# Reordering a top-256 search, three elementwise products and two loads in a two-layer trunk on Trainium2

## The chip, the cores and the metric

The kernel runs on one core of one Trainium2 chip. The metric is the device time of one execution in microseconds (us); lower is better. The number compared is the median of several executions.

## What is computed

The reference is a trunk of two layers over 1024 tokens of width 1024. Layer 0 projects its input into two groups of heads. Group A is RWKV-7 time mixing with eight heads of 64; group B is sparse attention with eight heads of 64, in which an indexer keeps for each query the 256 best keys. Layer 1 is gated linear attention. What the change touches is this part of layer 0, cut from the reference:

```python
kk = (k * kk_scale).reshape(Bn, T, H, Dh)
kk = kk / jnp.maximum(jnp.sqrt(jnp.sum(jnp.square(kk), -1, keepdims=True)), 1e-12)
k = k * (1.0 + (a - 1.0) * ka)
...
bonus = jnp.sum(r_h * k_h * rk, -1, keepdims=True) * v_h
...
score = jnp.where(adm[None], score, -jnp.inf)
vals, idx = lax.top_k(score, top_k)
```

The gates of both groups are SiLU of further columns of the same projection.

## The kernel before

**Projection.** Layer 0's input projection is computed 128 columns at a time: 21 column projections (`proj`, L527), each of 48 matmuls with 512 columns (three partial products L218 to L220 of split operands, two halves of the sequence) into one of two PSUM tiles called `dn`. A `dn` tile is drained by two instructions, one on ScalarE and one on VectorE: `shift_out` (L545 to L548) for r, k and v into one of three `sh` buffers, `gate` (L532 to L538) for a gate into the single `sg` buffer, which a DMA then stores to `d_gate`. TensorE can't start the projection after next before both drains are done. In the order of the program the last eight projections are v2, gate 4, gate 5, k3, v3, r3, gate 6 and gate 7; they are called the 14th to the 21st here. The digit of k3, v3 and r3 is the feature group j.

**Operands of the RWKV heads.** For each j from 0 to 3 and each half h of the sequence, `operands` (L606 to L634) makes the factors `ar` and `bk` of the chunked recurrence from r, k, the decays (L586 to L605) and the norms (`rn`, L570 to L584): L612, L615, L616, then kf (L619), k times kf (L620), L621, L622 and L623. `bk` is stored to `d_bk`, multiplied in place by PC (L628) and stored again to `d_bd`; r times k (L631, into a buffer called `kk`) feeds the `bonus` matmul (L637, one of 128x512 for each half), whose result VectorE takes up in L639. The table OG says for each kind of product up to which j it runs on GpSimd (POOL); on GpSimd a product runs in pieces of 128x256 by a helper whose line is L100.

**Search.** Beside the projections the threshold of the top 256 is searched for the score tiles 2 to 7 (128 queries each, 384 to 1024 keys). VectorE counts for tiles 3, 4 and 5 (`count_pass`, L738, 32 passes). ScalarE does tiles 2, 6 and 7 by sums of signs (`sign_pass`, L768 to L770): sixteen rounds on the upper 16 bits of the keys, a merge of both halves (nH, kd, L778 to L785), sixteen rounds on the rest. A round of one tile is a chain of three instructions. Then L794 to L801 turn the results into thresholds, for all of ScalarE's tiles at once, and the selection (L809 to L815) makes a mask from each tile in the order SELO.

**What sets the order.** A scheduler places the instructions of this part in each engine's queue; each engine then runs its queue strictly in that order. Behind the projection the second stage begins: the attention of tile i (`logits`: L915, L916 on TensorE, L917, L923 on VectorE, L925 on ScalarE; `weights`: L944) needs the queries `qT` of tile i, loaded by `load_q` (L899 to L902) into one of two buffers through SyncE's DMA queue (SP). Beside it run the recurrence's products (L1112 to L1116) on AT and BK, loaded through the same queue. Matmuls of this stage keep the order of the program.

Of the kernel before, what the change touches and what calls it, by code (L numbers as in the profile page):

```python
# [8 lines left out]
F32 = mybir.dt.float32  # L9
# [4 lines left out]
AF = mybir.ActivationFunctionType  # L14
ALU = mybir.AluOpType
# [6 lines left out]
P = 128  # L22
SEQ = 1024
# [36 lines left out]
PRE = ('', 'ab', 'cd!x', '0', '1lm', '', 'AB', 'CD!TX', '2', '3LM', '', '')  # L60
PO0 = 8
PINS = ()
SELO = (3, 4, 5, 2, 6, 7)
GNE = 'VVVV'
QSE = 'GG'
ATS = (2, 6, 7)
OG = (0, 0, 0, 0, 0, 0, 4, 4, 4, 0, 0)
ORD = (2, 3, 4, 9, 10, 5, 7, 11, 6, 8)
PG = [[], [0, 1], [], [], [2, 3], [4], [5], [6, 7], [], []]
RK1 = 0  # L70
# [11 lines left out]
def trunk(ctx: ExitStack, tc: tile.TileContext, x, positions, e_w_in, a_mu, a_w0, a_w2, a_a0, a_a2,  # L82
          a_kk_scale, a_ka, a_rk, a_gn_g, a_gn_b, b_kv_norm_g, b_wuk, b_wuv, e_w_out, o_w_in, c_g2,
          c_g_bias, c_norm_g, o_w_out, ln_g, ln_b, out, dbg=None, stop=None):
    nc = tc.nc
    V, A, G, PE = nc.vector, nc.scalar, nc.gpsimd, nc.tensor
    f32 = lambda ap: ap.bitcast(F32)
# [175 lines left out]
    d_q = dram.tile([NT, P, 8, P], F32, name="d_q")  # L263
# [79 lines left out]
    gt = gt_ctx.enter_context(tc.tile_pool(name="gt", bufs=1))  # L343
# [188 lines left out]
    def gate(z):  # L532
        g, j = divmod(z, 4)
        pt = proj((C_GB if g else C_GA) + j * P)
        o = gt.tile([P, SEQ], F32, name="sg")
        A.activation(o, pt, AF.Tanh, scale=0.5)
        V.scalar_tensor_tensor(o, o, 1.0, pt, op0=ALU.add, op1=ALU.mult)
        nc.sync.dma_start(d_gate[z], o)  # L538
# [22 lines left out]
    def st(name, w=SEQ, bufs=1, tag=None, pool=None):  # L561
        return (pool or t2).tile([P, w], F32, name=name, tag=tag or name, bufs=bufs)
# [149 lines left out]
    AT = ATS  # L712
# [4 lines left out]
    th = th_ctx.enter_context(tc.tile_pool(name="thr", bufs=1))  # L717
# [15 lines left out]
    def count_pass(b, last):  # L733


        for i in VT:
            z = col[i]
            V.tensor_scalar(junk[:, :P * (i + 1)], sc[:, rng(i)], Ff[:, z] if b < 31 else 0.0, None, op0=ALU.is_ge,  # L738
                            op1=ALU.add, accum_out=cnt[:, z])
        V.tensor_scalar(step, cnt, float(TOPK), float(1 << b) if b < 31 else -1.0, op0=ALU.is_lt, op1=ALU.mult)  # L740
        nxt = 1 << b >> 1
        if b == 31:
            V.tensor_scalar(F, step, nxt, None, op0=ALU.bitwise_xor)
        else:
            V.scalar_tensor_tensor(F, step, nxt, F, op0=ALU.bitwise_xor, op1=ALU.bitwise_xor)
# [14 lines left out]
    def half(i, z):  # L760
        return keys[i].bitcast(I16).rearrange("p (n z) -> p n z", z=2)[:, :, z]

    def sign_pass(b, data, c):


        for i in AT:
            zz = acol[i]
            A.activation(ajunk[:, :P * (i + 1)], data[i], AF.Sign, bias=c[:, zz], accum_out=cntA[:, zz])  # L768
            A.activation(sgA[:, zz], cntA[:, zz], AF.Sign, bias=odd[:, zz])
            A.activation(c[:, zz], sgA[:, zz], AF.Identity, scale=-0.5 * float(1 << b), bias=c[:, zz])  # L770
# [1 line left out]
    V.memset(Hc, 0.5)  # L772
    V.memset(Lc, 0.5)
    hi = {i: half(i, 1) for i in AT}
    for b in range(31, 15, -1):
        count_pass(b, False)
        sign_pass(b - 16, hi, Hc)
    V.tensor_scalar(nH, Hc, 131072.0, None, op0=ALU.mult)  # L778
    dist = {}
    for i in AT:  # L780
        n = P * (i + 1)
        d = th.tile([P, SEQ], F32, name="kd", tag="km", bufs=2)[:, :n]
        A.activation(d, hi[i], AF.Identity, scale=131072.0, bias=nH[:, acol[i]])
        dist[i] = keys[i].bitcast(F32)
        V.tensor_add(dist[i], d, half(i, 0))  # L785
    for b in range(15, -1, -1):
        count_pass(b, b == 0)
        sign_pass(b, dist, Lc)

    cand, nv = small("cand", NI), small("nv", NI)  # L790
    V.tensor_copy(cand[:, 0:ND], Ff)
# [107 lines left out]
    def load_q(i):  # L899
        if i < NT:  # L900
            QT_[i] = qp.tile([P, 8, P], F32R, name="qT", tag="qT", bufs=2)
            nc.sync.dma_start(f32(QT_[i]), d_q[i])  # L902

    def logits(i, h):

# [833 lines left out]
```

## Time and profile before

| what | value |
|---|---|
| median of 3 runs | 1267.45 us (1266.19 to 1272.92) |
| profiled execution | 1270.15 us, its span 1268.4 us |
| mean granted TensorE clock | 0.967 of full speed |
| TensorE busy | 1170.1 us, 92% of the span |
| VectorE, ScalarE, GpSimd busy | 60%, 50%, 34% of the span |

Times inside the profile are us from the start of the span. The span is 1.75 us shorter than the time of its own execution, and that execution was 2.7 us above the median. In the rows of the waits the last three numbers are the total wait, how often, and the longest.

### The profile page before, as it was taken

The numbers are of one execution on the slowest core, as the hardware profiler recorded it, in microseconds if no ns is written. First come the engines' busy times: TensorE is split into PE (matmuls) and PEld (weight loads), VectorE is DVE, ScalarE is ACT, GpSimd is POOL, SyncE is SP. The second block draws the span as 40 slices with busy tenths as digits, with TensorE's granted clock in tenths as the row PEclk, the third lists the DMA queues.
The fourth block names the chain that finished last, engine by engine and source line by source line (L and its number), as shares of the span: only waits on it lengthen the run. The fifth ranks groups of instructions, "written<-read, shape, count | busy, mean of one in ns | idle before, by whom it ended". The sixth has DMA issues, their size and how long they took to land.

```text
span 1268.4 us, 22109 instructions
## 1 busy us (share of the span) xinstructions
PE 1170.1 (92%) x8125; PEld 937.8 (74%) x8125; DVE 761.5 (60%) x1785; ACT 634.7 (50%) x1395; POOL 427.5 (34%) x741
## 2 busy tenths in 40 slices
PE   7998799989897968998988999999999999998997
PEld 6986587767675656777776777787788788886885
DVE  5245869989966666677776544882601034524666
ACT  5247859999882456666676421324811034413100
POOL 3233843536345333355454400513033130321000
PEclk9999899999998979999999999999999999998999
DMA  6102221535344475344454555852022020014221
GB/s 215 42 1 83 100 59 51 167 87 154 99 122 128 134 200 145 91 132 109 116 136 123 159 165 164 270 180 73 1 67 67 3 65 1 33 35 141 75 100 50
DMA packets 166096, 131.40 MB, mean 104 GB/s; under 512 B 61684, under 2 KB 139556, under 8 KB 165988
## 3 DMA queue, kind: packets, MB, share of 16 engines
q1 hardware_dynamic: 163152, 123.51, 33.4%
q10 hardware_dynamic: 2836, 6.49, 1.6%
q8 instruction: 64, 1.05, 0.4%
q14 instruction: 44, 0.36, 0.1%
HBM read 86.44 MB, written 42.99 MB: 102 GB/s over the span
## 4 chain that ended last, share of the span: by engine, by line
PE 61%; DVE 13%; ACT 10%; DMA 6%; issue 6%; POOL 4%; SPq 1%; DVEq 0%; ACTq 0%; POOLq 0%
PE op L858 7%; PE s L858 6%; PE dn L218 5%; PE dn L219 4%; PE dn L220 4%; DVE fe L738 3%; PE gt L242 2%; PE gt L240 2%; PE gt L241 2%; ACT fs L768 2%; PE s L944 2%; DMA wraw<-in_e_w_in_dram 2%; PE po L978 1%; PE tr L241 1%; PE tr L240 1%
## 5 line engine op out<-in xcount | busy, mean ns | idle before, releaser
L100 POOL TENSOR_TENSOR w<-qT,w 128x256 fp32r<-128x256 f32 x104 | 77.7, 782 | 210.1 <-ACT w L200 127.1
L218 PE MATMUL dn<-xh,chi 128*128 128x512 f32 x336 | 136.4, 406 | 8.7 <-DVE sh L547 7.3
L219 PE MATMUL dn<-xl,chi 128*128 128x512 f32 x336 | 133.9, 399 | 0.0
L220 PE MATMUL dn<-xh,clo 128*128 128x512 f32 x336 | 133.3, 397 | 0.0
L200 ACT CAST w<-qT 128x512 fp32r<-128x512 f32 x64 | 39.1, 622 | 106.1 <-PE dn L220 67.7
L218 PEld LDWEIGHTS dn<-xh,chi 128*128 128x128 f32 x336 | 64.2, 191 | 27.7 <-DVE sh L547 9.0
L738 DVE TENSOR_SCALAR_CACHE_REDUCE fe<-sc,F 128x512 bf16<-128x512 f32 (+2 forms) x93 | 81.6, 877 | 2.4
L219 PEld LDWEIGHTS dn<-xl,chi 128*128 128x128 f32 x336 | 64.2, 191 | 16.0 <-issue 3.1
L220 PEld LDWEIGHTS dn<-xh,clo 128*128 128x128 f32 x336 | 64.3, 191 | 14.1 <-issue 0.5
L100 POOL TENSOR_TENSOR clo<-craw,chi 128x256 fp32r<-128x256 f32 x84 | 73.2, 902 | 0.7
L858 PE MATMUL op<-w,yh 128*128 128x512 f32 x192 | 62.2, 411 | 1.4 <-ACT yh L1696 1.4
L925 ACT ACTIVATE w<-w,am 128x128 f32<-128x128 f32 (+7 forms) x64 | 49.6, 776 | 23.0 <-DVE am L923 22.8
L455 DVE SCALAR_TENSOR_TENSOR sc<-rl,wi_s,sc 128x384 f32<-128x384 f32 (+5 forms) x42 | 45.8, 1090 | 23.8 <-ACT rl L450 21.2
L944 PE MATMUL s<-ident,w 128*128 128x128 f32 x288 | 49.5, 298 | 9.2 <-ACT w L925 5.6
L100 POOL TENSOR_TENSOR vg<-vg,sg 128x256 f32<-128x256 f32 x32 | 23.7, 762 | 99.7 <-DVE vg L1661 53.6
L917 DVE CUSTOM_DVE_ANT_0 w<-s,bias_s 128x512 f32<-128x512 f32 (+1 forms) x80 | 45.3, 593 | 19.6 <-PE s L916 19.1
L228 POOL CAST chi<-craw 128x1024 fp32r<-128x1024 f32 x21 | 23.6, 1126 | 83.9 <-PE dn L219 54.6
L240 PE MATMUL gt<-w,hh 128*128 128x512 f32 x128 | 51.9, 406 | 0.0
L946 ACT COPY pT<-s 128x512 f32<-128x512 f32 x72 | 42.1, 586 | 18.7 <-PE s L944 17.6
L242 PE MATMUL gt<-w,hl 128*128 128x512 f32 x128 | 51.2, 400 | 0.0
L241 PE MATMUL gt<-w,hh 128*128 128x512 f32 x128 | 51.0, 399 | 0.0
L219 PE MATMUL dn<-hl,w 128*128 128x512 f32 x128 | 50.6, 395 | 0.0
(473 smaller groups left out, 3371.8 us busy)
## 6 DMA issues: line engine op xcount, KB each, us to landing
qT<-in_o_w_in_dram SPq DMA_DIRECT2D x48, 256.0 KB
craw<-in_e_w_in_dram SPq DMA_DIRECT2D x21, 512.0 KB
xt<-in_x_dram SPq DMA_DIRECT2D x8, 512.0 KB
d_q<-qiT SPq DMA_DIRECT2D x8, 512.0 KB
d_gate<-sg SPq DMA_DIRECT2D x8, 512.0 KB
d_ar<-ar SPq DMA_DIRECT2D x8, 512.0 KB
qT<-d_q SPq DMA_DIRECT2D x8, 512.0 KB
AT<-d_ar SPq DMA_DIRECT2D x32, 128.0 KB
```

What stands on the lines that cost most here:

```text
L100: return [f(out[:, a:min(n, a + w)], *(z[:, a:min(n, a + w)] for z in ins)) for a in range(0, n, w)]
L218: PE.matmul(pst, wh[:, cs], ah[:, k, sl], start=(k == 0), stop=False)
L219: PE.matmul(pst, wh[:, cs], al[:, k, sl], start=False, stop=False)
L220: PE.matmul(pst, wl[:, cs], ah[:, k, sl], start=False, stop=(k == NK - 1))
L240: PE.matmul(pst, ah[:, k, sl], wh, start=(k == 0), stop=False)
L241: PE.matmul(pst, ah[:, k, sl], wl, start=False, stop=False)
L242: PE.matmul(pst, al[:, k, sl], wh, start=False, stop=(k == NK - 1))
L455: E.scalar_tensor_tensor(acc[:, a:b], r, w, acc[:, a:b], op0=ALU.mult, op1=ALU.add)
L738: V.tensor_scalar(junk[:, :P * (i + 1)], sc[:, rng(i)], Ff[:, z] if b < 31 else 0.0, None, op0=ALU.is_ge, op1=ALU.add, accum_out=cnt[:, z])
L858: ins = PE.matmul(pt, a[:, k, :], b, start=(k == 0 and z == 0), stop=(k == NK - 1 and z == 2))
L925: A.activation(ps[k][:, :n], ps[k][:, :n], AF.Exp, scale=0.125, bias=m[:, k:k + 1], accum_out=rsum[:, k:k + 1])
L944: inorder(PE.transpose(pt[:, j * P:(j + 1) * P], OUT[i]["ps"][2 * j + s][:, kt * P:(kt + 1) * P], ident))
```

## The change

Four things change. (1) ScalarE first searches tiles 6 and 7 through all their rounds and then tile 2 alone; the merge is made for each tile by itself, and the rounds are spread evenly over the 32 counting passes. The selection takes tile 2 last. (2) Gate 7 is drained into an `sh` buffer instead of `sg`. (3) Three products leave GpSimd for VectorE: the product with PC (L628) and kf (L619) for j=3, and r times k (L631) for j=2 and j=3. A product with PC is then one VectorE instruction of 128x1024, r times k one of 128x512. (4) The queries of tiles 2 and 3 are loaded through ScalarE's DMA queue.

```diff
-SELO = (3, 4, 5, 2, 6, 7)
+SELO = (3, 4, 5, 6, 7, 2)
-ATS = (2, 6, 7)
-OG = (0, 0, 0, 0, 0, 0, 4, 4, 4, 0, 0)
+ATS = (6, 7, 2)
+ATL = (2,)
+LG = 7
+QA = (2, 3)
+OG = (0, 0, 0, 0, 0, 0, 3, 2, 3, 0, 0)
...
-        o = gt.tile([P, SEQ], F32, name="sg")
+        o = st("sh", bufs=3) if z >= LG else gt.tile([P, SEQ], F32, name="sg")
...
-    for b in range(31, 15, -1):
-        count_pass(b, False)
-        sign_pass(b - 16, hi, Hc)
-    V.tensor_scalar(nH, Hc, 131072.0, None, op0=ALU.mult)
...
+    early = [i for i in AT if i not in ATL]
+    steps = []
+    for tiles in (early, list(ATL)):
+        steps += [(sign_pass, b, hi, Hc, tiles) for b in range(15, -1, -1)] + [(halves, tiles)]
+        steps += [(sign_pass, b, dist, Lc, tiles) for b in range(15, -1, -1)]
+    for n, b in enumerate(range(31, -1, -1)):
         count_pass(b, b == 0)
-        sign_pass(b, dist, Lc)
+        for f, *a in steps[len(steps) * n // 32:len(steps) * (n + 1) // 32]:
+            f(*a)
...
-            nc.sync.dma_start(f32(QT_[i]), d_q[i])
+            (nc.scalar if i in QA else nc.sync).dma_start(f32(QT_[i]), d_q[i])
```

Lines of the changed kernel are 3 higher than before up to the search (L631 becomes L634) and 10 higher behind it (L796 becomes L806). The number of instructions on TensorE stays. The order of the queues differs from early in the search up to the first tiles of the second stage; behind that it is the same.

**First place: VectorE's queue at the second half of j=2.** Here `L620` to `L622` make k and bk, `L811` to `L814` are the selection of tile 7, `L547` drains a projection, and `L639` takes up the bonus. Before:

```order
L620 TENSOR_TENSOR sh<-sh,kf 128x512
L621 SCALAR_TENSOR_TENSOR tha<-tha,kk 128x512
L811 TENSOR_TENSOR need<-eqs,sums 128x1
L813 SCALAR_TENSOR_TENSOR E<-fe 128x1024
L623 TENSOR_TENSOR bk<-sh,thw 128x8x64
L622 TENSOR_TENSOR bk<-tha,thw 128x8x64
L814 SCALAR_TENSOR_TENSOR fe<-E,need,fs 128x1024
L547 SCALAR_TENSOR_TENSOR sh<-dn,par,sh 128x1023
L597 MEMSET ld 128x8
L639 TENSOR_TENSOR kk<-ix,sh 128x512
```

Of the changed kernel, from the same k times kf (now L623) on:

```order
L623 TENSOR_TENSOR sh<-sh,kf 128x512
L624 SCALAR_TENSOR_TENSOR tha<-tha,kk 128x512
L626 TENSOR_TENSOR bk<-sh,thw 128x8x64
L625 TENSOR_TENSOR bk<-tha,thw 128x8x64
L634 TENSOR_TENSOR kk<-sh 128x512
L550 SCALAR_TENSOR_TENSOR sh<-dn,par,sh 128x1023
L642 TENSOR_TENSOR kk<-ix,sh 128x512
```

The selection of tile 7 no longer stands between the products, and r times k (L634) is now VectorE's own. TensorE's bonus matmul of this half moved forward with it, from behind the 18th projection to behind the 20th of its 48 matmuls, and the first half's from behind the 21st matmul of the 17th projection to behind the 39th of the 16th.

**Second place: VectorE's queue in the 18th to 20th projection.** `Li` is the first instruction that needs the end of ScalarE's search, `rn` the norms of j=3. Before, the search had ended, and its selection been made, ahead of these rows:

```order
L639 TENSOR_TENSOR kk<-ix,sh 128x512
L653 TENSOR_SCALAR brk<-bones,par 128x128
L547 SCALAR_TENSOR_TENSOR sh<-dn,par,sh 128x1023
L581 TENSOR_SCALAR rn<-ix 128x512 x2
L598 TENSOR_SCALAR ld<-thw 128x8x64
L599 SCALAR_TENSOR_TENSOR ld<-m_1548,ld 128x520
L547 SCALAR_TENSOR_TENSOR sh<-dn,par,sh 128x1023
L612 SCALAR_TENSOR_TENSOR kk<-sh,par,rn 128x512 x2
```

Of the changed kernel:

```order
L584 TENSOR_SCALAR rn<-ix 128x512
L550 SCALAR_TENSOR_TENSOR sh<-dn,par,sh 128x1023
L806 TENSOR_SCALAR Li<-Lc 128x3
L807 SCALAR_TENSOR_TENSOR Hi<-Hi,Li 128x3
L808 TENSOR_SCALAR Li<-Hi 128x3
L809 TENSOR_TENSOR cand<-Hi,Li 128x3
L811 TENSOR_SCALAR nv<-cand 128x3
L820 TENSOR_SCALAR fe,eqs<-sc,cand 128x896
L820 TENSOR_SCALAR fe,eqs<-sc,cand 128x1024
L823 SCALAR_TENSOR_TENSOR E<-fe 128x896
L821 TENSOR_TENSOR need<-eqs,sums 128x1
L584 TENSOR_SCALAR rn<-ix 128x512
```

The thresholds of ScalarE's tiles and the selection of tiles 6 and 7 now stand between the first and the second half of the norms, and the selection of tile 2 follows, ahead of the drain (L550) of r3.

**Third place: the end of the projection.** VectorE's queue before, from gate 6's drain to the first logits (`cmask` is the causal mask):

```order
L537 SCALAR_TENSOR_TENSOR sg<-sg,dn 128x1024
L622 TENSOR_TENSOR bk<-tha,thw 128x8x64
L639 TENSOR_TENSOR kk<-ix,sh 128x512 x2
L894 MEMSET cmask 128x128
L895 MEMSET cmask 64x64
L537 SCALAR_TENSOR_TENSOR sg<-sg,dn 128x1024
L917 ISA w,mx<-s,cmask 128x128
L917 ISA mx 128x1
```

and of the changed kernel:

```order
L540 SCALAR_TENSOR_TENSOR sg<-sg,dn 128x1024
L626 TENSOR_TENSOR bk<-sh,thw 128x8x64
L625 TENSOR_TENSOR bk<-tha,thw 128x8x64
L634 TENSOR_TENSOR kk<-sh 128x512
L631 TENSOR_TENSOR bk<-bk,PC 128x1024
L642 TENSOR_TENSOR kk<-ix,sh 128x512
L631 TENSOR_TENSOR bk<-bk,PC 128x1024
L642 TENSOR_TENSOR kk<-ix,sh 128x512
L904 MEMSET cmask 128x128
L905 MEMSET cmask 64x64
L540 SCALAR_TENSOR_TENSOR sh<-sh,dn 128x1024
L927 ISA w,mx<-s,cmask 128x128
L927 ISA mx 128x1
```

The two products with PC (L631) now stand ahead of gate 7's drain. On ScalarE's queue of the changed kernel, from the gates' drains on:

```order
L539 ACTIVATE sg<-dn 128x1024
L539 ACTIVATE sh<-dn 128x1024
L935 ACTIVATE w,rsum<-w,am 128x128 x6
L912 DMA qT<-d_q 128x1024
L935 ACTIVATE w,rsum<-w,am 128x128 x2
L956 COPY pT<-s 128x512
L948 COPY rb<-rsum 128x512
```

The load of tile 2's queries stands between the exponentials of tile 0; before, no DMA stood there.

## Rows read from the trace of the kernel before

**Rows 1.** TensorE's waits, 380 to 480 us: what waited, for whom; total, times, longest.

```profile
PE ix L637 <- POOL kk L100: 5.8, 1, 5.8
PE s L944 <- ACT w L925: 5.6, 1, 5.6
PE s L915 <- DMA qT<-d_q: 5.3, 1, 5.3
PE s L915 <- DVE sg L537: 2.4, 1, 2.4
```

**Rows 2.** TensorE's timeline, 386 to 403 us: start, duration, instruction, [idle before it and releaser].

```profile
389.50 0.39 PE L219 MATMUL dn<-xl,chi 128*128 128x512 f32 x1
389.73 0.39 PE L220 MATMUL dn<-xh,clo 128*128 128x512 f32 x1
395.91 2.08 PE L637 MATMUL ix<-kk,brk 128*128 128x512 f32 x2 [5.79 <-POOL kk L100]
398.84 0.80 PE L218 MATMUL dn<-xh,chi 128*128 128x512 f32 x1 [0.86 <-DVE ld L597]
...
400.29 0.63 PE L218 MATMUL dn<-xh,chi 128*128 128x512 f32 x1
400.72 0.63 PE L219 MATMUL dn<-xl,chi 128*128 128x512 f32 x1
```

**Rows 3.** Busy time by stretch: PE, PEld, DVE, ACT, POOL, PE clock (1.00 is 2.4 GHz), DMA share.

```profile
360.00:380.00 20.00, 20.00 (x85) 15.30 (x84) 13.36 (x20) 16.22 (x42) 11.21 (x13) 1.00 0.62 182
380.00:400.00 20.00, 13.35 (x50) 9.53 (x49) 19.89 (x27) 8.96 (x16) 13.79 (x11) 0.88 0.56 169
400.00:420.00 20.00, 20.00 (x81) 14.54 (x79) 5.23 (x6) 7.22 (x9) 5.10 (x8) 0.95 0.20 50
...
460.00:480.00 20.00, 16.28 (x110) 13.50 (x111) 11.70 (x40) 10.57 (x27) 1.43 (x2) 0.83 0.92 237
```

**Rows 4.** GpSimd's timeline, 384 to 441 us.

```profile
392.01 3.84 POOL L100 TENSOR_TENSOR kk<-sh 128x256 f32<-128x256 f32 x2 [0.63 <-DVE tha L621]
...
440.42 1.18 POOL L100 TENSOR_TENSOR bk<-bk,PC 128x256 f32<-128x256 f32 x2 [2.57 <-DMA d_bk<-bk]
```

**Rows 5.** VectorE's timeline, 376 to 440 us.

```profile
379.63 0.61 DVE L810 TENSOR_SCALAR_CACHE_REDUCE fe<-sc,cand 128x384 bf16<-128x384 f32 x1
...
390.08 0.72 DVE L620 TENSOR_TENSOR sh<-sh,kf 128x512 f32<-128x512 f32 x1
...
396.32 1.27 DVE L814 SCALAR_TENSOR_TENSOR fe<-E,need,fs 128x1024 bf16<-128x1024 f32 x1
...
422.64 0.69 DVE L616 TENSOR_TENSOR ar<-sh,ld 128x512 f32<-128x512 f32 x1
```

**Rows 6.** TensorE's waits, 250 to 345 us.

```profile
PE dn L218 <- DVE sh L547: 7.3, 2, 3.7
```

**Rows 7.** ScalarE's timeline, 176 to 178 us: the first round of tile 2's search.

```profile
176.24 0.61 ACT L768 ACTIVATE fs<-key,Hc 128x384 bf16<-128x384 int16 x1
...
177.31 0.30 ACT L770 ACTIVATE Hc<-sgA,Hc 128x1 f32<-128x1 f32 x1
```

**Rows 8.** ScalarE's timeline, 368 to 376 us: the last round of the search.

```profile
369.65 0.62 ACT L768 ACTIVATE fs<-key,Lc 128x384 bf16<-128x384 f32 x1
...
370.62 1.05 ACT L768 ACTIVATE fs<-key,Lc 128x896 bf16<-128x896 f32 x1
...
374.30 0.31 ACT L770 ACTIVATE Lc<-sgA,Lc 128x1 f32<-128x1 f32 x1
```

**Rows 9.** SyncE's DMA queue, 434 to 464 us: start and duration of the issue.

```profile
436.21 0.60 SPq L568 DMA_DIRECT2D d_bk<-bk  x1
...
458.39 0.54 SPq L902 DMA_DIRECT2D qT<-d_q  x1
```

**Rows 10.** VectorE's timeline, 440 to 470 us.

```profile
442.34 1.22 DVE L537 SCALAR_TENSOR_TENSOR sg<-sg,dn 128x1024 f32<-128x1024 f32 x1 [0.65 <-ACT sg L536]
...
449.25 0.23 DVE L1046 TENSOR_SCALAR gn<-par 128x8 f32<-128x8 f32 x1 [3.07 <-DMA d_gate<-sg]
```

More of the change, by code (lines that the diff above doesn't have):

```diff
@@ L761, in half, with sign_pass @@
         return keys[i].bitcast(I16).rearrange("p (n z) -> p n z", z=2)[:, :, z]
-    def sign_pass(b, data, c):
-        for i in AT:
+    def sign_pass(b, data, c, tiles):
+        for i in tiles:
             zz = acol[i]
@@ L774, in trunk, with halves @@
     hi = {i: half(i, 1) for i in AT}
-    for b in range(31, 15, -1):
-        count_pass(b, False)
-        sign_pass(b - 16, hi, Hc)
-    V.tensor_scalar(nH, Hc, 131072.0, None, op0=ALU.mult)
     dist = {}
[L780 to L786, printed above, removed]
+    def halves(tiles):
+        for i in tiles:
+            zz = acol[i]
+            V.tensor_scalar(nH[:, zz], Hc[:, zz], 131072.0, None, op0=ALU.mult)
+            d = th.tile([P, SEQ], F32, name="kd", tag="km", bufs=2)[:, :P * (i + 1)]
+            A.activation(d, hi[i], AF.Identity, scale=131072.0, bias=nH[:, zz])
+            dist[i] = keys[i].bitcast(F32)
+            V.tensor_add(dist[i], d, half(i, 0))
+    early = [i for i in AT if i not in ATL]
[4 more added lines that the diff above has]
+    for n, b in enumerate(range(31, -1, -1)):
         count_pass(b, b == 0)
-        sign_pass(b, dist, Lc)
+        for f, *a in steps[len(steps) * n // 32:len(steps) * (n + 1) // 32]:
+            f(*a)
     cand, nv = small("cand", NI), small("nv", NI)
```

## The prediction

> **What bounds the kernel now.** I read the busy shares first, then TensorE's waits, then the timeline of each engine around the waits. TensorE is busy for most of the span, and every part that the change touches lies beside the input projection or right behind it. So a microsecond counts only where TensorE stands. The reader is to see in the list of waits that between 380 and 480 us it stands four times [rows 1]: 5.8 us for r times k on GpSimd, 5.6 us for an exponential of the attention, 5.3 us for a load of queries, 2.4 us for a drain of gate 7. Two more waits, 7.3 us together, lie earlier, for drains on VectorE beside the search [rows 6]. The sum of all of them is 26.4 us, about 2% of the time; with the slower clock behind some of them, no edit here can give much more.
>
> The first wait is the largest. TensorE's timeline [rows 2] shows its last projection matmul at 389.73, then nothing until 395.91, where both bonus matmuls run. The following matmul comes at 398.84 after another 0.86 us, and from there to 402 us matmuls start 0.43 us apart, where they started 0.23 apart before the gap: the granted clock fell to the lower of its two levels (1.2 in place of 2.4 GHz) after the engine had stood, and its mean in 380 to 400 us is 0.88 [rows 3]. Why it stood is in two other timelines. VectorE was busy 19.89 of those 20 us [rows 3]: the selection of ScalarE's three tiles runs from 379.63 to 397.6 [rows 5], and the products of j=2 wait in line with it, k times kf until 390.08 [rows 5]. Then GpSimd makes r times k in 3.84 us [rows 4], and only then can the bonus run.
>
> **The change part by part.** Costs are on the profiled execution.
>
> *Search order and r times k for j=2.* With tiles 6 and 7 first and tile 2 behind, ScalarE's search ends later, so its selection moves out of 380 to 397 us, and the products of j=2 pass it [first place of the change]. GpSimd's 3.84 us become one 128x512 product on VectorE, 0.69 us by the row of the same shape (at 422.64) [rows 5]. The bonus itself now stands 28 matmuls earlier, 28 x 0.23 = 6.4 us [rows 2]. VectorE can pay for that: it was idle 6.6 of the 20 us from 360 to 380 [rows 3], and the selection that filled the next 18 us is gone from there. Removed: 5.79 + 0.86 of waiting; the two bonus matmuls take 2.08 us where two at full clock take 1.02, 1.06 less; and eight matmuls cost 0.43 in place of 0.23, 1.6 less [rows 2]. Together **-9.3 us**. Bounds: -6.5 if the clock still falls from a small rest of the gap, -10 if the stretch closes wholly.
>
> *The two drains at 255 and 325 us* [rows 6] stay. The drain passes one count at the second, and two merges slip ahead of the first: 0, within 1 us either way.
>
> *The later end of the search.* The trace does not show tile 2's chain alone over sixteen rounds; its first round shows the three dependent steps, from 176.24 to 177.61, 1.38 us [rows 7], against 0.97 us per turn when the other tiles fill its gaps, 369.65 to 370.62 [rows 8]. So 32 rounds cost 32 x 0.41 = 13 us more, and the end goes from 374.6 [rows 8] to 388 us, and to some 395 when the drains and exponentials that ScalarE does in between are put into it. On VectorE the thresholds wait for that, and some 13 us of selection follow (the 18 us from 379.63 to 397.6 [rows 5] less seven products of j=2 at about 0.7 us) ahead of the second half of the norms of j=3 and of the drain of r3 [second place]. VectorE had 5.23 us of work in 400 to 420 us [rows 3], so most of it fits in; but TensorE needs the bank of the norms and the tanh of j=3 within that stretch. I put down three short waits of about 0.7 us, **+2.0 us**; bounds 0 (all hidden) and +8 (half of the selection is not hidden). I take a value near the lower end because the end of the search lies some 6 us ahead of the place in the 19th projection where the bank is next wanted, at about 401.
>
> *PC and r times k of j=3 on VectorE.* GpSimd's pieces go (the last at 440.42, after waiting 2.57 us for the store of bk [rows 4]). On VectorE the second product with PC (1.4 us, twice the row of 128x512 [rows 5]) waits for the same store, 4.2 us from its last issue at 436.21 [rows 4, 9], and queued behind it is now gate 7's drain, for which TensorE's first logits wait 2.4 us [rows 1]. GpSimd waited aside; VectorE waits in front [third place]. The bonuses of j=3 also come 12 and 14 matmuls later than before. So the drain at 442.34 [rows 10] starts 2 to 3 us later: **+2.4 us**; bounds 0 (the products of j=3 come as early as before, and the landing lies ahead of the projection's end) and +5 (the whole store is waited for).
>
> *Gate 7 in another buffer.* Nothing. It removes the wait of gate 7's drain for gate 6's store, but ScalarE waits there for TensorE anyway. The 5.6 us [rows 1] are the landing of gate 7's own store, on which VectorE waits 3.07 us until 449.25 [rows 10], with the maxima that the exponentials need queued behind it; the memory of the second stage is free only after that store, in whatever buffer the gate was.
>
> *Queries on ScalarE's queue.* Before, SyncE issues the load of tile 2 at 458.39 [rows 9], behind fourteen loads for the recurrence that could start only when that store had landed, and TensorE stands 5.3 us for it. On ScalarE's queue it stands behind six exponentials of tile 0, whose maxima come ahead of VectorE's wait that ends at 449.25 [rows 10]: at least 9 us earlier. So the wait goes, but the traffic does not: **-4.5 us**; bounds -5.3 and 0.
>
> Sum: -9.3 + 2.0 + 2.4 - 4.5 = **-9.4 us**. From the profiled 1270.15 that is 1260.7, from the median of 1267.45 it is 1258.0, which I take. Behind 495 us the order is the same, so the shift is carried to the end.
>
> **The rivals.**
>
> *All of the gain stays* (0.13). The two added waits don't occur, because VectorE has the time that rows 3 show: -9.3 - 4.5, about 1253 to 1254.
>
> *The load only changes places* (0.25). The DMA engines are 92% busy from 460 to 480 us [rows 3]. Queries loaded 9 us earlier take their time from gate 7's store or from AT, BK and BD, and TensorE stands for these instead, up to the same 5.3 us. With the two added waits at 3 us each the sum is -9.3 + 6 = -3.3, 1264: within 0.5%. Against it speaks that SyncE's queue, not the engines, held the load until 458.39 [rows 9]. The Trainium skill, "DMA: Bandwidth & Descriptors", section "Issuing engines are not separate DMA queues", says that loads issued from several engines interleave on the same sixteen DMA engines and that a second issuer saves only issue time. By that rule the load would win what it stood in line, 9 us, and no bandwidth; the trace agrees so far that the engines are nearly full there.
>
> *The search ends too late: slower* (0.12). VectorE's queue is strictly in order. If ScalarE's chain of tile 2, with other work in every gap, ends behind 401 us instead of 395, say at 403, the norms and the drain of r3 stand behind the thresholds and the 13 us of selection, and TensorE stands 2 us for the search, 1 for the thresholds' small instructions, 13 for the selection, and then loses 2.7 us at the lower clock as in rows 2. That is about 19 us against 9.3 + 4.5 - 2.4 = 11.4 won: +7.6, 1275. The point that decides is the end of the search against the 47th matmul of the 19th projection. For it speaks the thin margin of 6 us; against it, that ScalarE is busy only 8.96 of 20 us in 380 to 400 [rows 3].
>
> **How the numbers follow.** The forecast case has 0.50, with its own range of 1254 to 1262. A measurement of this kernel can tell about 0.5%, 6.3 us, from no change: faster is below 1261.1. All of the forecast but its upper edge, and the first rival: 0.60 faster. The second rival and that edge: 0.28 the same. The third: 0.12 slower, above 1273.8. The range reaches from 1251 (both bounds of gain) to 1270, which leaves out most of the third rival and little else.
>
> **What would show it.** Right: no wait of TensorE for `kk` near 390 us, its clock near 1.00 there; r times k at 0.7 us on VectorE ahead of the bonus; the end of the search near 395 us; the wait for qT gone; a longer wait for gate 7's drain. The forecast is wrong if TensorE's waits in 395 to 430 us come to more than 8 us, if the wait for qT comes back as one for AT or BK, or if the second stage is as late as before though the projection ended earlier.

## The result, and the profile after

The changed kernel took **1257.38 us** (median of 8 runs, 1255.26 to 1264.14) against 1267.15 us (8 runs, 1264.25 to 1272.92) of the kernel before on the same chip: ratio **0.992**, 95% interval 0.9894 to 0.9945, so 9.8 us faster by the medians. The forecast was 9.4 us and 1258.0. The profiled execution took 1257.07 us with a span of 1255.3 us at a mean granted clock of 0.977 (before: 1270.15, 1268.4, 0.967).

TensorE's waits from 380 to 442 us, the stretch of [rows 1] up to the second stage (what waited, for whom; total, times, longest):

```profile
PE s L925 <- DVE sh L540: 3.9, 1, 3.9
PE ix L640 <- DVE kk L634: 1.4, 1, 1.4
PE ix L596 <- DVE rn L584: 1.0, 1, 1.0
PE ix L596 <- ACT thw L598: 0.3, 1, 0.3
```

The 5.8 us for GpSimd's r times k are gone. A shorter wait of 1.4 us for VectorE's r times k has come in, at j=3 (it ends at 427.90), and the drain of gate 7 takes 3.9 us in place of 2.4. The waits of after from 442 to 500 us:

```profile
PE s L954 <- ACT w L935: 4.0, 1, 4.0
PE x L1190 <- DVE Tn L1185: 3.9, 1, 3.9
...
PE g L1122 <- DMA AT<-d_ar: 0.4, 1, 0.4
```

The 5.3 us for qT are gone, and no wait of that size for AT or BK took their place. The exponential (L954 in place of L944 in [rows 1]) is waited for 4.0 us, not 5.6. Two earlier places belong to the sum too. The waits of after from 240 to 345 us:

```profile
PE dn L221 <- DVE sh L550: 4.9, 2, 2.7
PE ix L640 <- POOL kk L103: 1.9, 2, 1.7
```

and from 345 to 380 us:

```profile
PE ix L596 <- DVE kk L642: 0.7, 1, 0.7
```

The two drains of [rows 6] shrank from 7.3 to 4.9 us. The windows of after (stretch, length, then busy time of PE, PEld, DVE, ACT and POOL with their counts, PE clock, DMA share, GB/s) show where VectorE's selection went:

```profile
360.00:380.00 20.00, 19.28 (x80) 14.34 (x79) 19.22 (x26) 14.43 (x37) 12.72 (x14) 1.00 0.56 160
380.00:400.00 20.00, 20.00 (x82) 15.06 (x81) 7.99 (x13) 17.24 (x49) 8.10 (x12) 1.00 0.57 143
400.00:420.00 20.00, 18.66 (x80) 13.87 (x80) 19.51 (x28) 14.98 (x22) 1.91 (x3) 1.00 0.27 81
```

Against [rows 3], TensorE is busy for all of 380 to 400 us at the full clock (13.35 us at 0.88 before), VectorE only 7.99 us of it (19.89), and VectorE's full stretch lies at 400 to 420 now (19.51 against 5.23).

To see where time goes, the same point of the program is read in both profiles. The end of the projection is the start of its last matmul plus 0.23 us, the spacing of [rows 2].

| point of the program | before | after | difference |
|---|---|---|---|
| end of the projection | 441.1 | 434.5 | -6.6 |
| first logits of tile 0 | 443.6 | 438.6 | -5.0 |
| first logits of tile 2 | 463.7 | 452.5 | -11.2 |
| first product of the solution (L1180, now L1190) | 501.1 | 492.1 | -9.0 |
| first matmul of the output projection on y (L858, now L868) | 710.3 | 701.2 | -9.1 |
| first matmul `gt` of layer 1 (L240, now L243) | 1017.1 | 1006.1 | -11.0 |

The whole gain was made by 492 us, and 209 us later it was still there. What comes between 701 us and the first `gt` takes 302.9 to 306.8 us in profiles of one order (the last column of the next table), so the medians count for the end.

The -6.6 us at the end of the projection have three parts. `dn` takes 1280 matmuls up to there, the last eight projections being the last 384 of them, and TensorE runs the same number of matmuls in each of these stretches in every profile of this case:

| stretch, by matmuls into `dn` | before | after | difference |
|---|---|---|---|
| first to 641st (249 us) | 243.15 | 242.85 | -0.3 |
| 641st to 1001st (356 us), past the two drains of [rows 6] | 107.33 | 106.02 | -1.3 |
| 1001st to 1280th, from the start of the 16th projection to the end of the 21st | 84.39 | 79.34 | -5.0 |

What the change does to j=2 and j=3 lies in the last stretch. It is the steadiest measure here: the three profiles with the old search and its old loop (before, e5, e6) take 84.1 to 84.5 us for it.

### The profile page after: what moved, and what is told of

Its sections match the earlier page's. It is cut to its first block, busy times and chain, and to the rows that moved or that the text cites. A ratio compares the mean times of both kernels' runs of the same rounds, so it can differ in the third digit from the quotient of the medians.

```text
span 1255.3 us, 22100 instructions
## 1 busy us (share of the span) xinstructions
PE 1165.0 (93%) x8125; PEld 934.3 (74%) x8125; DVE 764.7 (61%) x1795; ACT 640.5 (51%) x1395; POOL 409.2 (33%) x723
## 4 chain that ended last, share of the span: by engine, by line
PE 54%; DVE 15%; DMA 9%; issue 8%; ACT 7%; POOL 4%; SPq 2%; DVEq 0%; ACTq 0%; POOLq 0%
PE op L868 7%; PE s L868 5%; DVE fe L741 4%; PE dn L221 4%; PE dn L222 4%; PE dn L223 4%; PE gt L245 2%; PE gt L244 2%; PE gt L243 2%; DMA wraw<-in_e_w_in_dram 2%; PE s L954 1%; PE tr L244 1%; PE tr L243 1%; PE tr L245 1%; PE po L988 1%
## 5 line engine op out<-in xcount | busy, mean ns | idle before, releaser
L103 POOL TENSOR_TENSOR clo<-craw,chi 128x256 fp32r<-128x256 f32 x84 | 69.9, 862 | 0.8
L868 PE MATMUL op<-w,yh 128*128 128x512 f32 x192 | 60.4, 399 | 1.7 <-ACT yh L1706 1.7
L954 PE MATMUL s<-ident,w 128*128 128x128 f32 x288 | 48.9, 296 | 8.9 <-ACT w L935 4.0
L243 PE MATMUL gt<-w,hh 128*128 128x512 f32 x128 | 51.9, 406 | 0.0
L221 PE MATMUL dn<-hh,w 128*128 128x512 f32 x128 | 50.6, 395 | 0.0
```

Of the source, the lines that this page charges most:

```text
L103: return [f(out[:, a:min(n, a + w)], *(z[:, a:min(n, a + w)] for z in ins)) for a in range(0, n, w)]
L221: PE.matmul(pst, wh[:, cs], ah[:, k, sl], start=(k == 0), stop=False)
L243: PE.matmul(pst, ah[:, k, sl], wh, start=(k == 0), stop=False)
L868: ins = PE.matmul(pt, a[:, k, :], b, start=(k == 0 and z == 0), stop=(k == NK - 1 and z == 2))
L954: inorder(PE.transpose(pt[:, j * P:(j + 1) * P], OUT[i]["ps"][2 * j + s][:, kt * P:(kt + 1) * P], ident))
```

## The experiments

Twelve variants were run, each compared with runs of the kernel before on its own chip. A ratio below 1 is faster than before; after has 0.992. The table also gives the last of the three stretches above ("16th to 21st"), and for the two questions of the second stage the time from the end of the projection to the first product of the solution (60.0 us before, 57.6 after), and the time from the first output matmul on y to the first `gt` matmul. The end of the projection is a poorer measure than the stretch: after and e8 have one order of work and are 2.2 us apart at the 641st matmul already, long before the place of their one difference.

| variant | median us | ratio, 95% interval | 16th to 21st | projection ends | to the solution | y to `gt` |
|---|---|---|---|---|---|---|
| before (profile) | | 1 | 84.4 | 441.1 | 60.0 | 306.8 |
| after | 1257.38 | 0.992, 0.9894 to 0.9945 | 79.3 | 434.5 | 57.6 | 304.9 |
| e1_search_as_before | 1276.44 | 1.0051, 1.0026 to 1.0077 | 82.1 | 442.9 | 55.1 | 319.8 |
| e2_products_as_before | 1261.97 | 0.9944, 0.9917 to 0.9971 | 81.4 | 437.4 | 58.9 | 304.3 |
| e3_loads_on_sync_queue | 1269.88 | 1.0005, 0.9989 to 1.0022 | 79.5 | 436.3 | 63.0 | 310.3 |
| e4_only_loads | 1279.58 | 1.0073, 1.0046 to 1.01 | 82.1 | 447.0 | 55.9 | 314.4 |
| e5_loads_alone | 1269.42 | 0.9993, 0.9972 to 1.0014 | 84.5 | 442.1 | 60.7 | 302.9 |
| e6_products_alone | 1266.58 | 0.9981, 0.9959 to 1.0003 | 84.1 | 440.7 | 59.7 | 305.1 |
| e7_search_alone | 1273.79 | 1.0025, 1.0004 to 1.0047 | 80.8 | 434.5 | 62.0 | 310.5 |
| e8_gate_in_sg | 1256.36 | 0.9894, 0.9864 to 0.9924 | 79.3 | 435.7 | 60.0 | 303.1 |
| e9_pc_on_gpsimd | 1261.03 | 0.9924, 0.9896 to 0.9953 | 79.8 | 435.6 | 62.6 | 305.1 |
| e10_late_gnp | 1261.15 | 0.9925, 0.9908 to 0.9941 | 79.1 | 434.7 | 58.1 | 306.1 |
| e11_setup_on_gpsimd | 1266.47 | 0.9974, 0.9958 to 0.999 | 78.7 | 434.4 | 64.0 | 304.7 |
| e12_thresholds_apart | 1270.54 | 0.9993, 0.9968 to 1.0018 | 82.9 | 438.9 | 56.5 | 313.8 |

**A trap in this table.** In e1, e3, e4, e7 and e12 the scheduler also put layer 0's output projection in another order (from 755 to 761 us on), some 300 us behind the edit in e3 and further in the others. In those five the last column reads 310 to 320 us, in all the others 303 to 307. TensorE's waits of e3 from 690 to 1030 us show some that after does not have:

```profile
PE x L1310 <- DVE Y L1294: 2.9, 1, 2.9
...
PE ca L1251 <- ACT TT L1221: 2.4, 1, 2.4
...
PE po L253 <- DVE hl L257: 1.3, 1, 1.3
```

The same stretch of after:

```profile
PE ca L1265 <- DVE RUV L1252: 3.5, 2, 2.0
PE ca L244 <- POOL w L103: 1.9, 2, 1.5
```

The waits for Y and hl come with the other order of e3, which e7 shares (3.2 and 1.6 us there); the wait for TT is not peculiar to it, since before has one of 4.3 us. The other three have orders of their own. The medians of those five kernels therefore say little of the edit itself, and their profiles are read only up to the first product of the solution.

**e8_gate_in_sg:** after with gate 7 back in `sg`.

```diff
-LG = 7
+LG = 8
```

> The changed kernel with gate 7 in sg again; the order of every queue is the same. My theory (the store of gate 7 holds the second stage in whatever buffer it is): the end of the projection, the wait for gate 7's drain (3.9 us) and the product at 492 us are all within 0.7 us of the changed kernel; median within 3 us of it. Rival (gate 7's drain was also held by gate 6's store): the drain comes 1 us or more later, and the second stage with it.

Measured 0.9894 (0.9864 to 0.9924), the same as after within the intervals; the drain wait is 4.0 us against 3.9. The buffer of gate 7 costs nothing that can be told, as forecast: ScalarE's half of the drain is released by TensorE's last matmul here too, not by gate 6's store. The profile missed its expectation all the same. The first product of the solution comes at 495.7, 3.6 us later than in after, where 0.7 was allowed; the median is not slower. Since each engine's order of work is that of after here, the two profiles show how far single profiles part: 2.2 us by 249 us, and 2.4 us (60.0 against 57.6) from the projection's end to the solution.

**e2_products_as_before:** after with all products of OG on GpSimd again.

```diff
-OG = (0, 0, 0, 0, 0, 0, 3, 2, 3, 0, 0)
+OG = (0, 0, 0, 0, 0, 0, 4, 4, 4, 0, 0)
```

> The changed kernel with the three products back on GpSimd; the new search, gate 7's buffer and the two loads stay. Theory A (the selection held the bonus): the wait for r times k of j=2 stays below 2 us, the projection ends within 2 us of the changed kernel's 435 us, and the wait for gate 7's drain falls from 3.9 to about 2.4 us; median 1255 to 1259. Theory B (the product on GpSimd held it): a wait of 3 us or more for r times k of j=2, and the projection ends at 438 us or later; median 1260 to 1264.

Measured 0.9944. TensorE's waits of e2, 380 to 442 us:

```profile
PE s L925 <- DVE sh L540: 2.4, 1, 2.4
PE ix L596 <- DVE rn L584: 2.3, 1, 2.3
PE ix L640 <- POOL kk L103: 1.3, 2, 1.2
```

The wait for r times k is 1.3 us although GpSimd makes it, over two bonuses. So the new search order by itself removes most of the 5.8 us, and the stretch from the 16th to the 21st projection falls from 84.4 to 81.4 us. What the products on VectorE add can hardly be told from the medians: 0.24% (0.9944 against 0.992) with intervals that overlap. In the stretch it shows: 79.1 to 79.5 us in the four profiles with all three products on VectorE and the order of after up to there (after, e3, e8, e10), 81.4 here and 80.8 in e7 below, both with the old products, so 1.3 to 2.3 us. The projection's end at 437.4 missed the expectation by little, but 2.2 us of it were there at 249 us. The median lies in theory B's range; the wait that theory B asks for is not there.

**e6_products_alone:** before with the products of j=3, and r times k of j=2, on VectorE, nothing else.

```diff
-OG = (0, 0, 0, 0, 0, 0, 4, 4, 4, 0, 0)
+OG = (0, 0, 0, 0, 0, 0, 3, 2, 3, 0, 0)
```

> The kernel before with only the three products on VectorE. Theory A (the selection in VectorE's queue held the bonus of j=2): a wait of 4 us or more for r times k stays and the projection ends within 3 us of before, and the wait for gate 7's drain grows from 2.4 to about 4 us; median 1265 to 1270. Theory B (GpSimd's product held it): the wait falls below 1.5 us, the projection ends 6 to 9 us earlier; median 1259 to 1263.

Measured 0.9981 (0.9959 to 1.0003). Its largest wait in 380 to 442 us:

```profile
PE ix L637 <- DVE kk L631: 6.0, 1, 6.0
```

and the product that ends it, on VectorE's timeline (start, duration):

```profile
395.12 0.68 DVE L631 TENSOR_TENSOR kk<-sh 128x512 f32<-128x512 f32 x1
```

The product itself takes 0.68 us in place of 3.84 [rows 4], but it starts at 395.12, 3.1 us later than GpSimd started its own at 392.01, because it stands in VectorE's queue, in line with the selection. GpSimd's slower product was not what held the bonus: the selection was. The moved products are worth 1.3 to 2.3 us only when the selection is out of their way (e2, e7). One expectation failed: the wait for gate 7's drain stays at 2.4 us, though the products with PC are on VectorE here. The second of them has ended at 439.3, ahead of the projection's end at 440.7; in after it ends at 436.5, behind the end at 434.5.

**e7_search_alone:** after with products, gate and loads as before.

```diff
-LG = 7
-QA = (2, 3)
-OG = (0, 0, 0, 0, 0, 0, 3, 2, 3, 0, 0)
+LG = 8
+QA = ()
+OG = (0, 0, 0, 0, 0, 0, 4, 4, 4, 0, 0)
```

> Only the new search, with the products on GpSimd, gate 7 in sg and the loads on SyncE's queue. Theory A (the selection held the bonus): the wait for r times k of j=2 is at most 2 us, the projection ends 3 to 6 us earlier than before, the wait for gate 7's drain is 2.4 us and the one for qT 5 us again; median 1262 to 1266. Theory B: a wait of 3 us or more for r times k stays and the projection ends within 2 us of before.

The projection ends at 434.5, where it ends in after, but by another sum. The stretch from the 16th projection on is 3.6 us shorter than in before (80.8 us), against 5.0 in after. The stretch before it, with the two drains, is 2.9 us shorter (104.4 against 107.3), against 1.3 in after: the drains are waited for as long in both, but the granted clock of 320 to 332 us stays at 1.00 in e7, where it is 0.86 in after and in before. So the search carries most of the gain up to the projection's end, and the products the rest. The qT wait of 4.9 us is still there and 62.0 us pass to the solution. The median, 1.0025, is far from the expected one; it holds the other order of the output projection. e2 differs from e7 in the loads and the gate's buffer only, and has 58.9 us to the solution, 3.1 less, in single profiles.

**e1_search_as_before** and **e4_only_loads:** the old table of tiles in the new loop; e4 has old products and gate as well (LG 8, OG 4, 4, 4).

```diff
-SELO = (3, 4, 5, 6, 7, 2)
-ATS = (6, 7, 2)
-ATL = (2,)
+SELO = (3, 4, 5, 2, 6, 7)
+ATS = (2, 6, 7)
+ATL = ()
```

> The changed kernel with the search as before: ScalarE's three tiles together and the selection in the order 3, 4, 5, 2, 6, 7; the products stay on VectorE, gate 7 in its other buffer, the two loads on ScalarE's queue. Theory A (the selection in VectorE's queue held the bonus of j=2): TensorE waits 5 to 7 us for r times k near 390 us, the slower clock behind it is back, and the projection ends within 3 us of the kernel before (441 us); median 1262 to 1266. Theory B (GpSimd's slow product held it): that wait is below 1.5 us and the projection ends near 435 us as in the changed kernel; median 1256 to 1260.

> The kernel before with the two loads on ScalarE's queue and nothing else. Theory A (the queue held the load): no wait for qT, the second stage at 500 us is 3 to 5 us earlier than before; median 1262 to 1264.5. Rival (the load only changes places): the second stage at 500 us is within 1.5 us of before; median 1265.5 to 1268.

Both edits did more than they were meant to: with an empty late group the loop still spreads the empty steps over the counting passes, and so lays all of ScalarE's rounds beside the first half of them. The drains at 240 to 345 us then wait longer than in before, 7.9 us with 4.3 the longest in both, and the projection ends at 442.9 and 447.0. Both lose the output projection's order on top. What stands is the waits for r times k: 4.0 us in e1, less than the 5 to 7 expected, and 3.6 in e4 (for GpSimd's). Selection ahead of the products brings the wait back, on whichever engine the product runs. For the loads, e5 took the place of e4.

**e5_loads_alone:** before, with only the two loads moved.

```diff
-            nc.sync.dma_start(f32(QT_[i]), d_q[i])
+            (nc.scalar if i in (2, 3) else nc.sync).dma_start(f32(QT_[i]), d_q[i])
```

> The kernel before, with its own search code, and only the loads of the queries of tiles 2 and 3 on ScalarE's queue. TensorE's order is the same, so the end of the projection is within 0.5 us of before. Theory A (SyncE's queue held the load): the wait of 5.3 us for qT is gone and the first product of the solution at 501 us comes 3 to 5.5 us earlier; median 1262 to 1265 against 1267 of before. Rival (the load only changes places with AT, BK and BD): that product is within 1.5 us of before; median within 1.5 us.

Measured 0.9993 (0.9972 to 1.0014): nothing. The wait for qT is gone; what is left of such size from 442 to 500 us:

```profile
PE s L944 <- ACT w L925: 4.7, 1, 4.7
PE s L915 <- DVE sg L537: 2.4, 1, 2.4
PE s L915 <- DVE g L968: 2.3, 1, 2.3
```

and from 500 to 560 us:

```profile
PE x L1180 <- DVE Tn L1175: 7.5, 1, 7.5
```

The solution's first product starts at 502.8 us against 501.1, after waiting 7.5 us for `Tn`; before it waited 3.7. The chain of waits of e5 shows why:

```profile
454.82 5.67 DMA BD<-d_bd
460.51 6.40 DMA g<-d_gate
466.94 0.70 DVE g L968
...
474.07 5.55 DMA d_m<-md
479.64 0.47 SPq L1135
480.16 4.58 DMA Mt<-d_m
```

The recurrence's loads BD and g and its round trip through `d_m` set the solution's start, and qT is not among them. In before the same round trip reads:

```profile
476.73 4.58 DMA d_m<-md
481.88 2.31 DMA Mt<-d_m
```

In e5 it starts 2.7 us earlier and ends no earlier (484.7 against 484.2): its two transfers take 10.1 us in place of 6.9. The gap that qT left is waited for 40 us later. Of the 1.7 us by which the solution starts later, 1.0 were there at the end of the projection, with TensorE's order unchanged, where 0.5 was allowed.

**e3_loads_on_sync_queue:** after with the two loads back on SyncE's queue.

```diff
-QA = (2, 3)
+QA = ()
```

> The changed kernel with the queries of tiles 2 and 3 back on SyncE's queue; all else stays up to the output projection of layer 0, where some matmuls of the output change places. Theory A (the queue held the load): the wait of TensorE for qT is back with 4 to 5.5 us and the second stage at 500 us is 3 to 5 us later than in the changed kernel; median 1260 to 1263. Rival (the load only changes places with AT and BK): the second stage at 500 us is within 1.5 us of the changed kernel; median 1256 to 1259.

The qT wait returns, 5.4 us, and the wait for `Tn` is 5.8 us (3.9 in after). From the projection's end to the solution it takes 63.0 us against 57.6, or 60.0 in e8, which has the order of after: the loads are worth 3.0 to 5.4 us there, in single profiles, which part by 2.4 us in this measure without any edit; e2 against e7 gave 3.1. Two pairs point the same way, but the size is not settled. The median, 1.0005, also holds some 5 us of the other output order.

**e9_pc_on_gpsimd:** after with the product with PC of j=3 back on GpSimd.

```diff
-OG = (0, 0, 0, 0, 0, 0, 3, 2, 3, 0, 0)
+OG = (0, 0, 0, 0, 0, 0, 4, 2, 3, 0, 0)
```

> The changed kernel with the product with PC of j=3 on GpSimd again, nothing else; TensorE's order stays. My theory (the two products with PC stand ahead of gate 7's drain and wait for the store of bk): the wait for gate 7's drain falls from 3.9 to 2.4 us, the landing of gate 7's store comes 1 to 1.5 us earlier against the end of the projection, and the median is 0 to 2 us below the changed kernel. Rival (GpSimd's eight pieces end later than VectorE's two products and the stores of bk with them): the drain is earlier, but the second stage still waits as long, for the stores that follow; median 0 to 3 us above the changed kernel.

Measured 0.9924 (0.9896 to 0.9953), the same as after within the intervals, which reach some 3.5 us to either side. The drain waits 2.4 us again (3.9 in after), and the next wait takes more than that back (442 to 500 us):

```profile
PE s L954 <- ACT w L935: 9.4, 1, 9.4
PE x L1190 <- DVE Tn L1185: 4.4, 1, 4.4
```

The chain of waits of e9 (start, duration):

```profile
438.16 0.33 PE s L925
441.41 7.13 DMA d_gate<-sh
448.69 0.55 SPq L1107
```

and that of after:

```profile
438.56 0.33 PE s L925
439.83 3.69 DMA d_gate<-sh
444.26 0.63 SPq L1060
```

The store of gate 7, 512 KB in both, took 7.13 us against 3.69, and SyncE's issues follow it at 448.69 against 444.26. The timelines of e9 show what stands around that store, on GpSimd, SyncE's queue and ScalarE's queue:

```profile
436.31 2.33 POOL L103 TENSOR_TENSOR bk<-bk,PC 128x256 f32<-128x256 f32 x4 [1.12 <-DVE cmask L905]
438.67 0.47 SPq L569 DMA_DIRECT2D d_bd<-bk  x1
441.55 0.35 ACTq L912 DMA_DIRECT2D qT<-d_q  x1
```

Counted from the end of the projection, gate 7's drain is done 1.5 us earlier than in after, but its store starts 0.5 us later (5.8 us behind the end against 5.3): in SyncE's queue the stores `d_bd` of GpSimd's last pieces stand ahead of it. The queries' load on ScalarE's queue did come earlier with the drain, 5.9 us behind the end against 7.4. So it starts within 0.2 us of the store, 512 KB beside 512 KB; in after it starts 2.0 us behind it. The landing was expected 1 to 1.5 us earlier and came 3.9 us later (12.9 us behind the end against 9.0). The rival describes what happened.

**e10_late_gnp:** after with four small loads (gnp, L1060) issued behind the loads of the second unit of the recurrence.

```diff
-    for z in range(2):
-        for s in range(2):
-            nc.sync.dma_start(gnp[RS[z], :, :, s], ...
+    def load_gn():
+        ...
...
+        if u == 1:
+            load_gn()
```

> The changed kernel with the four small loads of the norm's weights (gnp, 1 KB each, 2.6 us of SyncE's queue) issued behind the loads of the second unit in place of between the first loads of AT. My theory (after gate 7's store SyncE's queue is the chain that ends last): the loads of BK and BD are issued 2.6 us earlier, and the first product of the solution at 492 us comes 1.5 to 3 us earlier; median 1254 to 1256.5 where the changed kernel has 1257.4. Rival (the landing of the transfers, not their issue, sets that time): it comes within 1 us; median within 1 us of the changed kernel.

Measured 0.9925 (0.9908 to 0.9941), no better than after. Both waits stay: 4.1 us for the exponential (4.0 in after) and 7.2 us for `Tn` (3.9). The first product of the solution comes at 492.8 against 492.1, as the rival has it. The four small loads were not what delayed the rest.

**e11_setup_on_gpsimd:** e10 with the product with PC on GpSimd, and the small constants and zeros of the second stage there too.

```diff
-    V.tensor_scalar(gn8, par[:, GNG:GNG + 8], 0.5, None, op0=ALU.mult)
+    G.tensor_scalar(gn8, par[:, GNG:GNG + 8], 0.5, None, op0=ALU.mult)
...
-            V.memset(ZS[z][RS[1 - s], :, s, :], 0.0)
+            G.memset(ZS[z][RS[1 - s], :, s, :], 0.0)
```

> The kernel with the late small loads, in which also the product with PC of j=3 is on GpSimd, and the setup of the second stage (the norm's weights, the zeros of RUV and Zs) is GpSimd's. VectorE then no longer waits in its own queue for the landing of gate 7's store ahead of the last maxima. My theory: the wait of 4.0 us for an exponential is gone or below 1.5 us; as the chain of loads sets the end, the second stage gains less than that, 1 to 3 us against the kernel with late loads alone; median 1252 to 1255. Rival (the exponentials' wait is hidden by that chain anyway): no gain over it.

Measured 0.9974, slower than after. The wait for the exponential is down to 0.3 us, since VectorE's setup, which had waited for the store, is on GpSimd. The time is waited for elsewhere, 442 to 500 us:

```profile
PE x L1195 <- DVE Tn L1190: 6.9, 1, 6.9
PE s L925 <- ACT pT L956: 6.8, 1, 6.8
```

Gate 7's store takes 7.0 us here too; the queries' load starts 0.6 us ahead of it.

**e12_thresholds_apart:** after with the thresholds of tiles 6 and 7 computed apart, so that they don't wait for tile 2.

```diff
-    V.tensor_scalar(Hi, Hc, -1.0, None, op0=ALU.mult)
...
+    ne = len(early)
+    for g in [slice(0, ne), slice(ne, NA)]:
+        h_, l_, c_ = Hi[:, g], Li[:, g], ci[:, g]
+        V.tensor_scalar(h_, Hc[:, g], -1.0, None, op0=ALU.mult)
...
```

> The changed kernel with the thresholds of tiles 6 and 7 computed apart from tile 2's, so that their selection no longer waits for the end of tile 2's search; a part of the order of the output projection of layer 0 changes too, so what counts is the projection's end. My theory (the selection behind the late end of the search makes TensorE's waits in the j=3 stretch): the waits between 390 and 430 us fall from 2.7 us to below 1.2 us and the projection ends 1 to 2.5 us earlier than in the changed kernel (434.5 us). Rival (the 13 us of selection only move to where VectorE is full): the waits come at the bonus of j=2 near 385 us instead, and the projection ends within 1 us of the changed kernel or later.

The waits at the norms and the bonus of j=3 fall away, and a larger one returns at j=2 (waits of 345 to 440 us):

```profile
PE ix L640 <- DVE kk L634: 4.9, 1, 4.9
```

VectorE's timeline of e12 has the selection of a large tile ahead of the product:

```profile
383.05 2.27 DVE L825 TENSOR_TENSOR_SCAN E<-fe 128x1024 f32<-128x1024 bf16 x1
...
390.54 1.21 DVE L634 TENSOR_TENSOR kk<-sh 128x512 f32<-128x512 f32 x1
```

The projection ends at 438.9, 4.4 us later than in after. So the common wait for tile 2, which reads like a flaw, is what keeps the selection behind the products of j=2.

## Why the prediction was right

**The total and its halves.** The sum, -9.4, stands against -9.1 at 701 us and -9.8 by the medians, and the main mechanism is shown. How close the halves came is partly luck. The step up to the end of the projection was forecast at -9.3 + 2.0 = -7.3 us and measured -6.6; but the stretch that holds these two terms gave -5.0, the two drains gave -1.3 that the forecast had at nothing, and 0.3 were there at 249 us. The second stage was forecast at +2.4 - 4.5 = -2.1 and measured -2.4 (-9.0 at the solution less -6.6); e8, with the same order of work, shows 0.0 there, so a single profile can't confirm that number.

**Search order and r times k for j=2, -9.3.** The mechanism is right. VectorE's timeline of after has the product at 381.51, the bonus follows without a wait at 383.15, and the clock of the stretch is 1.00 (start, duration, instruction, [idle before it and releaser]):

```profile
381.51 0.69 DVE L634 TENSOR_TENSOR kk<-sh 128x512 f32<-128x512 f32 x1
...
398.15 0.86 DVE L806 TENSOR_SCALAR Li<-Lc 128x3 int32<-128x3 f32 x1 [1.09 <-ACT Lc L773]
...
405.40 0.68 DVE L584 TENSOR_SCALAR rn<-ix 128x512 f32<-128x512 f32 x1
...
414.95 1.28 DVE L550 SCALAR_TENSOR_TENSOR sh<-dn,par,sh 128x1023 f32<-128x1023 f32 x1
```

The forecast gave the two causes in one term; e2, e6 and e7 part them. The new search order alone shortens the stretch by 3.0 to 3.6 us (e2, e7). The move to VectorE without it gives 0.3 (e6, with 6.0 us of waiting left), and with it another 1.3 to 2.3.

**The two drains, 0 within 1.** Missed in size: 4.9 us in place of 7.3, so -2.4, of which 1.1 went to the bonus at GpSimd's r times k (1.9 us; 0.8 in e5, where the search is that of before). Net -1.3 in after; -2.9 in e7, where the clock did not fall behind the second drain.

**The later end of the search, +2.0.** The mechanism is right, the size too small. ScalarE's timeline of after shows tile 2's rounds alone:

```profile
388.44 0.62 ACT L771 ACTIVATE fs<-key,Lc 128x384 bf16<-128x384 f32 x1
...
389.84 0.62 ACT L771 ACTIVATE fs<-key,Lc 128x384 bf16<-128x384 f32 x1
...
397.82 0.29 ACT L773 ACTIVATE Lc<-sgA,Lc 128x1 f32<-128x1 f32 x1
```

A round takes 1.40 us (1.38 forecast), and the search ends at 398.1, not 395. With the selection behind the thresholds at 398.15, the norms of j=3 come at 405.40 and r3's drain at 414.95. TensorE's waits behind it are 1.0, 0.3 and 1.4, 2.7 us together where three of 0.7 were forecast; e12 removes these three by parting the thresholds. A fourth, 0.7 us at 370 us, lies ahead of the search's end and stays in e12 (0.8): VectorE is fuller there (19.22 us of 360 to 380 against 13.36), which the forecast left out. With all four, 3.4 us, the forecast's own -9.3 would make the stretch 5.9 us shorter; it is 5.0 shorter, and the last 0.9 is not accounted for. The third rival had its point at 401 us: the search came 3 us short of it.

**PC and r times k of j=3 on VectorE, +2.4.** This is the term that failed. The drain did grow, by 1.5 us (3.9 against 2.4). With the same products on VectorE it stays at 2.4 in e6, e1 and e12, where the products of j=3 come early enough: the term's own lower bound. And the term took a later drain for lost time, but the next wait fell with it: the 5.6 us for the exponential became 4.0. e9 undoes the product with PC: the drain's 1.5 us come back, the next wait is 9.4 us, and 62.6 us pass to the solution against 57.6. By the profiles the sign turned at the load that the same change moved: with the drain earlier and the store of gate 7 not, the queries' load and the store start together. No run tests that by itself. The medians of e9 and after (0.9924 and 0.992) exclude neither 0 nor +2.4, so the price of the term stays open.

**The loads, -4.5.** The wait went as forecast. SyncE's queue had held the load of tile 2 until 458.39 [rows 9]; ScalarE issues it 16.5 us earlier:

```profile
441.87 0.35 ACTq L912 DMA_DIRECT2D qT<-d_q  x1
```

Whether its time went too depends on what else comes early. Within the change, undoing it costs 3.0 to 5.4 us up to the solution (e3), little above what two profiles of one order part by. Alone it gains nothing (e5): the second rival, that the load only changes places, describes what e5 did, though the stall came back for `Tn` rather than for AT, BK or BD. Its other branch, that the load takes its time from gate 7's store, fits e2, e9 and e11. The Trainium skill, "DMA: Bandwidth & Descriptors", section "Issuing engines are not separate DMA queues", says that transfers issued from several engines interleave on the same 16 DMA engines and that only issue time is saved. In e5 the load is issued 10.0 us earlier and the time stays (0.9993), which agrees. How much of after's -9.8 us belongs to the loads stays open: no run has the new search, the old loads and after's order of the output projection.

**The gate's buffer, 0.** Right (e8).

## What to carry to other kernels

When an engine runs its queue in order, ask what stands ahead of an operation in it before asking which engine is faster at it: here a product over five times as fast (0.68 us for 3.84), moved alone, gained nothing that can be told, and 1.3 to 2.3 us once the selection no longer stood ahead of it. Price a wait together with the wait behind it, since the first one that is removed may be paid at the next, as for `Tn` in e5; and ask which transfer an earlier one will run beside. And where a scheduler places the work, an edit undone may reorder a stage hundreds of microseconds away; compare the same points of the program in both profiles before reading anything out of a median.

## What was not expected of the hardware

The store of gate 7, 512 KB each time, took 3.1 to 7.1 us to land. The spread goes with the load of tile 2's queries, 512 KB too:

| load issued, counted from the store's issue | store lands after |
|---|---|
| 0.6 us ahead (e11), 0.1 behind (e9), 0.4 behind (e2) | 7.0, 7.1, 5.2 us |
| 1.6 to 2.9 us behind (e4, after, e1, e10, e12, e8, e5) | 4.5, 3.7, 3.2, 4.2, 3.7, 4.2, 4.3 us |
| on SyncE's queue, over 12 us behind (before, e3, e6, e7) | 4.3, 4.0, 3.1, 4.0 us |

In all fourteen profiles the store takes over 5 us only where the load starts within 0.6 us of it. No run moves the load alone by so little, so this is read off, not tested. In this kernel a forecast that rests on a landing should ask what else is issued at that moment, and carry the range for either case.
